# 320 series of products of zeros ahead of a hybrid decoder step: what distances of the operands modulo 512 bytes cost

## The chip, the cores and the metric

The kernel runs on one core of one Trainium2 chip. The metric is the device time of one execution in microseconds (us). A core has TensorE (PE; matmuls, with a weight load ahead of each), VectorE (DVE), ScalarE (ACT), GpSimd (POOL) and SyncE (SP, which issues most DMAs). Operands lie in SBUF, in 128 partitions; products go to PSUM.

## The reference

One inference step of a hybrid decoder trunk with one layer, for a prompt of 512 tokens and 8 samples of 8 tokens, 576 tokens in all with 1024 features:

```python
u = _rms(x) * g_pre_mix
proj = u @ w_in                                   # Mamba2-SSD heads and mLSTM heads, one projection
...
x = x + _rms(mix) * g_post_mix
u = _rms(x) * g_pre_x                             # cross attention to a memory of 256 rows
...
x = x + _rms(o) * g_post_x
u = _rms(x) * g_pre_ffn
f = (jax.nn.silu(u @ w_gate) * (u @ w_up)) @ w_down
x = x + _rms(f) * g_post_ffn
```

It returns the new x of both groups, the memory's keys and values, and the states of the scans. All of it is in float32.

## The kernel before

All activations are held with features on partitions and the 576 tokens along the free dimension, eight tiles of 128 features each. To keep float32 accuracy, both the activation and the weight of a large product are split into a rounded high part and a low part (type float32r), and a product is made of three matmuls: high weight by high activation, high weight by low activation, low weight by high activation. The 576 tokens are taken in two parts, either 256 and 320 or 288 and 288; the products of values per token are 512 wide, with the activation as the 128-column operand and the weight as the moving one.

`build` writes the layer down in order, and a scheduler settles the order of the instructions on each engine by its own simulation, within the constraints that the code gives (`issue_after`, `high_priority`, `manual_schedule`, which fixes the written order).

What stands around the change is the beginning. Line 300 clears a small tile `wz`; line 303 issues 21 products of it (`ps_warm`), which nobody reads; line 304 loads the parameters. Then the eight feature tiles of x are loaded, and ScalarE and VectorE make their high parts `uh` (L322) and low parts `ul` (L323) as they come, and `split` (L191, L192) does the same for the two first weight tiles, `whi` and `wlo`. The first stage, lines 339 to 341, multiplies them as they become ready: 8 feature tiles by 2 weight tiles by 2 parts of the tokens by 3 matmuls, 96 products:

```python
mm(ps, wh, ah, start=k == 0, stop=False)
mm(ps, wh, al, start=False, stop=False)
mm(ps, wl, ah, start=False, stop=k == KT - 1)
```

Behind it `gemm` (L202, L203, L205) does the same for the other tiles of the projection, and the later stages follow: values (L815), output projection (L202 to L205, `ps_o`), cross attention, and the feed-forward products (L1846 to L1848).

`SL(slot, ...)` takes one of the large slots of SBUF, 18,432 bytes in each partition; slot 1 is first used by `qk` (L470) in the kernel before. `MP` takes one of three rotating PSUM tiles, of one bank each.

Of the kernel before, what the change touches and what calls it, by code (L numbers as in the profile page):

```python
# [11 lines left out]
F32 = mybir.dt.float32  # L12
F32R = mybir.dt.float32r
# [6 lines left out]
P = 128  # L20
# [95 lines left out]
def build(nc, tc, ctx, I, O):  # L116
    V, A, G, S, TE = nc.vector, nc.scalar, nc.gpsimd, nc.sync, nc.tensor
    mm = TE.matmul
# [12 lines left out]
    def SL(slot, name, dt=F32, shape=(P, KT, T)):  # L131

        return big.tile(list(shape), dt, name=name, tag="s%d" % slot, bufs=1)
# [5 lines left out]
    def MP(name="m"):  # L139
        return pa.tile([P, 512], F32, name=name, tag="a")  # L140
# [54 lines left out]
    def gemm(ps, units, xh, xl, t0, n, k0=0, k1=None, order=None, late=0):  # L195


        tiles = [(hi[:, j * P:(j + 1) * P], lo[:, j * P:(j + 1) * P]) for hi, lo, nk in units for j in range(nk)]
        order = order or range(len(tiles))
        for i, k in list(enumerate(order))[k0:k1]:  # L200
            (wh, wl), ah, al = tiles[k], xh(k, t0, n), xl(k, t0, n)
            mm(ps, wh, ah, start=i == 0, stop=False)  # L202
            mm(ps, wh, al, start=False, stop=False)  # L203
            for c in range(late) if i == late - 1 else [i] if i >= late else ():
                m = mm(ps, tiles[order[c]][1], xh(order[c], t0, n), start=False, stop=c == len(tiles) - 1)  # L205
        return m
# [94 lines left out]
    psw = MP("ps_warm")  # L301
    for _ in range(NWARM):
        mm(psw[:, 0:256], wz[:, 0:128], wz, start=True, stop=True, skip_group_check=True)
    S.dma_start(par, I["par"])

    wi = [[wp.tile([P, 1024], F32R, name=k, tag=k, bufs=3) for k in ("whi", "wlo")] for _ in range(2)]
# [46 lines left out]
    stop = gemm(ps0[2][1], [(*w2, KT)], U, UL, 256, 320, 0, NSS)  # L353
# [12 lines left out]
    stop = gemm(ps0[3][0], [(*w3, KT)], U, UL, 0, 256)  # L366
# [343 lines left out]
    for g in range(2):  # L710
        psb = BP("ps_ls")
        pb3 = psb.rearrange("p (h t) -> p h t", h=8)
        for h in range(8):
            mm(psb[:, h * TS:(h + 1) * TS], sel[:80, 8 * g + h:8 * g + h + 1].to_broadcast([80, P]), cumst[:, TP:T],
               start=h == 0, stop=h == 7, skip_group_check=True)
# [8 lines left out]
        for h in range(8):  # L724
            k, j = h % 2, (8 * g + h) // 2
            mm(psi[64 * k:64 * k + 64, j * TS:(j + 1) * TS], xdts[:, 8 * g + h, :], lm[:, h, :], start=True, stop=True,
               skip_group_check=True)
# [12 lines left out]
    for b in range(4):  # L740
# [3 lines left out]
        for g in range(2):  # L744
            for hb in (1, 0):
# [3 lines left out]
                   start=b == 0, stop=b == 3, skip_group_check=True)  # L749
        for hb in range(2):  # L750
            bb, hn, (bst, xst) = 4 * hb + b, hns[hb], hbs[hb]
            bm = sd.tile([96, 256], F32R, name="bm", tag="bm", bufs=1)
# [136 lines left out]
    for h in range(4):  # L889
        q, k = qk[:, h, :], qk[:, 4 + h, :]  # L890
# [5 lines left out]
        dm = mp_.tile([P, 512], F32, name="dm", tag="dm", bufs=2)  # L896
# [5 lines left out]
        for c in range(4):  # L902
            mm(pss[:, c * P:(c + 1) * P], k[:, c * P:(c + 1) * P], q[:, c * P:(c + 1) * P], start=True, stop=True,
               skip_group_check=True)
# [39 lines left out]
    for h in range(4):  # L944
        mm(psb[:, h * TS:(h + 1) * TS], sel[:68, h:h + 1].to_broadcast([68, P]), sxst[:, TP:T], start=h == 0, stop=h == 3,
           skip_group_check=True)
# [22 lines left out]
    for hb in range(2):  # L969
# [6 lines left out]
        for b in range(4):  # L976
# [3 lines left out]
            for h in range(4):  # L980
                mm(psn[32 * h:32 * h + 32, 0:257], qpad[:, h, bb, :], c0[:, h, 0:257], start=False, stop=b == 3,
                   skip_group_check=True)
# [241 lines left out]
    x = SL(1, "x1")  # L1224
# [267 lines left out]
    def xo(j, i, pool=None):  # L1492

        t0, n = EHALVES[i]

        with tc.issue_after(evx[j - 3].ins if j > 2 else ovs[5].ins):
            ps, w = GP("ps_xo")[:, :n], weights(("xo", j), I["wxo"][j], pool=pool, cut=1024)

        def step(k0, k1):
            m = gemm(ps, [(*w, KT)], act(oh), act(ol), t0, n, k0, k1, [2, 3, 4, 5, 6, 7, 0, 1], 6 if j == 3 else 0)  # L1500
            if k1 < KT:
                return m
            add_sq(ph, ssq, ps, j if i == 0 else XO1.index(j), n, t0=t0)
            evx.append(A.activation(f[:, j, t0:t0 + n], ps, AF.Copy, scale=PAR("g_postx", j)))
            return m, evx[-1]
        return step
# [10 lines left out]
    for j in range(8):  # L1517
        step = xo(j, 0, wx if 3 < j < 7 else None)
# [662 lines left out]
    parts = [(c, d) for c in range(2) for d in range(2)]  # L2181
# [172 lines left out]
```

## Time and profile before

| | |
|---|---|
| median of 2 runs | 1088.56 us (1088.47 to 1088.65) |
| the profiled execution | 1087.01 us, of which the span from the first to the last instruction is 1085.2 us |
| mean granted TensorE clock | 0.998 |
| instructions on PE | 8124 matmuls, 8124 weight loads |
| moved from and to HBM | 160.28 MB read, 20.65 MB written |

The span is what the profile shows of one execution. In its rows, PE is a matmul, PEld a weight load; the two overlap, and matmuls overlap each other as well, so that a row's duration is longer than the distance to the next row. "L202" is line 202 of the kernel; "ps_in<-uh,whi" names what is written and read; "x24" is a count. In the rows of stretches, an engine's count takes in every instruction that lies in the stretch with any part of it.

### The profile page before, as it was taken

The page shows a single profiled execution, that of the slowest core. Times are in us where ns is not written, and L with a number is a line of the kernel's source. Part 1 is how long each engine was busy: PE and PEld are TensorE (multiplying, and loading weights), DVE is VectorE, ACT ScalarE, POOL GpSimd, SP SyncE. Part 2 cuts the span into 40 slices and gives each one's busy share as a digit, 9 for nine tenths or more (in the row PEclk, how much of TensorE's full clock was granted, in tenths as well). Part 3 has the DMA queues.
Part 4 walks back from the last instruction along what each step waited for, and adds up shares of the span by engine and source line. Part 5 has one row for each costly group of instructions (what it writes and reads, how often), then busy time and mean ns, then how long its engine had stood idle before and what let it go on. Part 6 is the DMA issues. An engine that isn't in the chain of part 4 may idle for free.

```text
span 1085.2 us, 20708 instructions
## 1 busy us (share of the span) xinstructions
PE 1075.0 (99%) x8124; PEld 1022.1 (94%) x8124; DVE 752.4 (69%) x1507; ACT 610.9 (56%) x1098; POOL 228.0 (21%) x305
## 2 busy tenths in 40 slices
PE   9999999999999999999999999999999999999997
PEld 9999887778999999999999989999999999999997
DVE  6896785658877775568755546766467887787556
ACT  7867632355654555656555545645566566656653
POOL 1332643313113111000154301100011111111000
PEclk9999999999999999999999999999999999999999
DMA  6775535435654449653458775643486697578532
GB/s 211 179 159 126 161 111 172 165 80 185 190 152 144 110 123 324 226 193 101 152 194 288 271 252 180 239 133 92 135 176 137 159 203 163 117 189 184 125 131 88
DMA packets 58966, 182.29 MB, mean 168 GB/s; under 512 B 6604, under 2 KB 11852, under 8 KB 58356
## 3 DMA queue, kind: packets, MB, share of 16 engines
q1 hardware_dynamic: 42740, 138.06, 38.6%
q0 software_dynamic: 15552, 41.95, 19.6%
q8 instruction: 64, 1.05, 0.4%
q10 hardware_dynamic: 576, 0.95, 0.3%
q14 instruction: 34, 0.28, 0.1%
HBM read 160.28 MB, written 20.65 MB: 167 GB/s over the span
## 4 chain that ended last, share of the span: by engine, by line
PE 86%; DVE 5%; ACT 4%; issue 2%; DMA 2%; POOL 0%; DVEq 0%; SPq 0%; ACTq 0%; POOLq 0%
PE ps_in L203 4%; PE ps_in L202 4%; PE ps_in L205 4%; PE ps_v L815 3%; PE ps_o L205 3%; PE ps_o L203 3%; PE ps_g L1846 3%; PE ps_g L1847 3%; PE ps_o L202 3%; PE ps_u L1847 3%; PE ps_u L1848 3%; PE ps_u L1846 3%; PE ps_g L1848 3%; PE ps_dn L1846 2%; PE ps_dn L1847 2%
## 5 line engine op out<-in xcount | busy, mean ns | idle before, releaser
L202 PE MATMUL ps_in<-uh,whi 128*128 128x320 f32 (+1 forms) x544 | 162.9, 300 | 0.5 <-DVE cb L451 0.5
L205 PE MATMUL ps_in<-uh,wlo 128*128 128x320 f32 (+1 forms) x544 | 162.3, 299 | 0.3 <-DMA wlo<-win 0.3
L203 PE MATMUL ps_in<-ul,whi 128*128 128x320 f32 (+1 forms) x544 | 161.8, 298 | 0.0
L180 ACT CAST whi<-raw 128x1024 fp32r<-128x1024 f32 (+1 forms) x104 | 105.2, 1013 | 100.0 <-PE ps_in L203 25.9
L187 DVE TENSOR_TENSOR wlo<-raw,whi 128x512 fp32r<-128x512 f32 (+1 forms) x96 | 93.7, 978 | 75.1 <-ACT whi L180 74.0
L202 PEld LDWEIGHTS ps_in<-uh,whi 128*128 128x128 f32 x544 | 102.8, 189 | 3.3 <-issue 1.7
L205 PEld LDWEIGHTS ps_in<-uh,wlo 128*128 128x128 f32 x544 | 102.3, 188 | 1.5 <-DMA wlo<-win 0.5
L203 PEld LDWEIGHTS ps_in<-ul,whi 128*128 128x128 f32 x544 | 102.4, 188 | 0.6
L185 POOL DMA_DIRECT2D wlo<-win x32 | 27.8, 869 | 80.7 <-ACT wlo L184 70.0
L1847 PE MATMUL ps_g<-b,whi 128*128 128x288 f32 x144 | 42.5, 295 | 0.0
L1846 PE MATMUL ps_g<-b,whi 128*128 128x288 f32 x144 | 42.4, 295 | 0.0
L1847 PE MATMUL ps_u<-b,whi 128*128 128x288 f32 x144 | 42.4, 295 | 0.0
L1846 PE MATMUL ps_u<-b,whi 128*128 128x288 f32 x144 | 42.2, 294 | 0.0
L1819 ACT CAST whi<-rawx 128x1024 fp32r<-128x1024 f32 (+1 forms) x26 | 25.6, 984 | 27.9 <-PE ps_dn L1847 13.8
L192 DVE TENSOR_TENSOR wlo<-sw,whi 128x1024 fp32r<-128x1024 f32 (+1 forms) x26 | 29.6, 1140 | 14.9 <-ACT whi L191 14.8
L202 PE MATMUL ps_xo<-qh,whi 128*128 128x288 f32 x128 | 38.5, 303 | 0.2 <-ACT whi L180 0.2
L205 PE MATMUL ps_o<-mixm_h,wlo 128*128 128x256 f32 (+1 forms) x128 | 37.9, 296 | 0.0
L1798 ACT CAST whi<-raw 128x1024 fp32r<-128x1024 f32 (+1 forms) x26 | 25.6, 983 | 21.8 <-PE ps_g L1847 9.7
L203 PE MATMUL ps_xo<-ql,whi 128*128 128x288 f32 x128 | 37.8, 296 | 0.0
L205 PE MATMUL ps_o<-mixs_h,wlo 128*128 128x320 f32 (+1 forms) x128 | 37.7, 295 | 0.0
L203 PE MATMUL ps_o<-mixs_l,whi 128*128 128x320 f32 (+1 forms) x128 | 37.7, 295 | 0.0
L203 PE MATMUL ps_o<-mixm_l,whi 128*128 128x256 f32 (+1 forms) x128 | 37.7, 295 | 0.0
(769 smaller groups left out, 3853.6 us busy)
## 6 DMA issues: line engine op xcount, KB each, us to landing
raw<-win SPq DMA_DIRECT2D x35, 512.0 KB, 4.0
raw<-wout SPq DMA_DIRECT2D x17, 512.0 KB, 3.7
raw<-wxq SPq DMA_DIRECT2D x13, 512.0 KB, 6.0
raw<-wgate SPq DMA_DIRECT2D x13, 512.0 KB, 3.6
raw<-wup SPq DMA_DIRECT2D x13, 512.0 KB, 5.1
wlo<-win POOLq DMA_DIRECT2D x24, 256.0 KB, 5.1
kva<-vc SPq DMA_DIRECT2D x11, 512.0 KB, 5.0
raw<-wv SPq DMA_DIRECT2D x10, 512.0 KB, 4.0
```

Source lines behind the costliest of these rows:

```text
L180: casts.append(A.copy(hi[:, :n], raw[:, :n]))
L185: G.dma_start(lo[:, a:b], src[:, a:b], accum_op=ALU.add)
L187: e.tensor_tensor(lo[:, a:b], raw[:, a:b], hi[:, a:b].bitcast(F32), op=ALU.subtract)
L192: (eng or V).tensor_tensor(lo, src, hi.bitcast(F32), op=ALU.subtract)
L202: mm(ps, wh, ah, start=i == 0, stop=False)
L203: mm(ps, wh, al, start=False, stop=False)
L205: m = mm(ps, tiles[order[c]][1], xh(order[c], t0, n), start=False, stop=c == len(tiles) - 1)
L815: mm(ps, a, b, skip_group_check=True, **kw)
L1798: s.c1 = A.copy(s.h1[:, s.all], s.r1[:, s.all])
L1846: mm(ps, wh, b[0][k], start=start and k == 0, stop=False, skip_group_check=True)
L1847: mm(ps, wh, b[1][k], start=False, stop=False, skip_group_check=True)
L1848: m = mm(ps, wl, b[0][k], start=False, stop=k == nk - 1, skip_group_check=True)
```

## The change

Ahead of the load of the parameters, VectorE clears a tile `bench` of 4608 float32 elements in each partition (slot 1), and PE is given 320 segments of products of it. All go to one PSUM tile, which nobody reads. Nothing is removed, and no other line is touched.

```diff
     for _ in range(NWARM):
         mm(psw[:, 0:256], wz[:, 0:128], wz, start=True, stop=True, skip_group_check=True)
+
+    bench = SL(1, "bench", F32R, (P, 4608))
+    V.memset(bench.bitcast(F32), 0.0)
+    SEG = []
+    for a in (0, 16, 32, 48):
+        for bm in range(8):
+            for dm in range(8):
+                if dm < 4 or not 0 <= a // 16 + (bm + 4) % 8 - 4 < 4:
+                    SEG.append((a, bm, dm, 576, ((320, 12), (256, 12), (320, 12), (256, 12), (288, 18), (512, 9))))
+    for a in (0, 16):
+        for bm in range(8):
+            for dm in range(8):
+                SEG.append((a, bm, dm, 288, ((288, 24),)))
+    pq = MP("ps_probe")
+    with tc.manual_schedule(engines={TE.engine}):
+        for a, bm, dm, step, parts in SEG:
+            for n, count in parts:
+                for i in range(count):
+                    k = i // 3 % (4 if step == 576 else 8)
+                    x = 64 + step * k + (a + 16) % 64 + (16 * bm + (1024 if step == 576 else 1152) if i % 3 == 1 else 0) + (256 if n == 320 else 0)
+                    w = 3600 + (16 * dm + 384 if i % 3 == 2 else 0)
+                    if n == 512:
+                        mm(pq[:, 0:n], bench[:, x:x + P], bench[:, w:w + n], start=i < 1, stop=True, skip_group_check=True)
+                    else:
+                        w += 128 * (k % 4)
+                        mm(pq[:, 0:n], bench[:, w:w + P], bench[:, x:x + n], start=i < 1, stop=True, skip_group_check=True)
     S.dma_start(par, I["par"])
```

Each segment copies the pattern of the kernel's own products, three at a time (i % 3): weights at w with the operand at x, the same weights with a second operand, other weights with the first operand. An element has 4 bytes, so 16 elements are 64 bytes and 128 are 512. Modulo 512 bytes, `a` sets the place of the first operand against the weights, `bm` that of the second operand against the first, `dm` that of the second weights against the first, each in steps of 64 bytes. The step of 576 or 288 elements from one threesome to the next moves the operand by 256 or 128 bytes modulo 512. At 512 columns the roles are exchanged: 128 columns at x are loaded as weights, and 512 from w are streamed.

The diff moves the later lines down by 26: L339 of before is L365 after.

## Prediction

> **What bounds the kernel now.** I read the page first: the span, the busy shares and the chain that ended last.
>
> ```profile
> span 1085.2 us, 20708 instructions
> ...
> PE 1075.0 (99%) x8124; PEld 1022.1 (94%) x8124; DVE 752.4 (69%) x1507; ACT 610.9 (56%) x1098; POOL 228.0 (21%) x305
> ```
> ```profile
> PE 86%; DVE 5%; ACT 4%; issue 2%; DMA 2%; POOL 0%; DVEq 0%; SPq 0%; ACTq 0%; POOLq 0%
> ```
>
> TensorE (PE) is occupied 1075.0 of 1085.2 us and holds 86% of the chain, so the first question is whether it has gaps in which further products could run. The view of waits, restricted to PE, answers it; these are its three longest.
>
> ```profile
> PE ps_warm L303 <- DVE wz L300: 1.1, 1, 1.1
> PE ps_in L202 <- DVE cb L451: 0.5, 1, 0.5
> PE ps_in L205 <- DMA wlo<-win: 0.3, 1, 0.3
> ```
>
> Behind the start, no wait is longer than 0.5 us. There is no gap to hide anything in: whatever is put into PE's queue ahead of the first stage moves all that follows by its own length. So the prediction is a count of products times the pace at which PE takes them.
>
> The pace has to be read with care. Busy time divided by the count would be wrong, since matmuls overlap: a row of the timeline shows how long one product was under way, but the next starts well before that has passed. The pace is the distance from start to start. Here are pairs of rows of PE's timeline, the first row of a series of equal products and the row that follows its last.
>
> ```profile
> 461.93 0.28 PE L202 MATMUL ps_o<-mixm_h,whi 128*128 128x256 f32 x1
> ...
> 464.75 0.31 PE L202 MATMUL ps_o<-mixm_h,whi 128*128 128x320 f32 x1
> ...
> 468.27 0.31 PE L202 MATMUL ps_o<-mixm_h,whi 128*128 128x320 f32 x1
> ...
> 471.50 0.28 PE L228 MATMUL ps_ss<-c,ssqm 128*128 128x1 f32 x2
> ...
> 841.23 0.29 PE L1846 MATMUL ps_g<-b,whi 128*128 128x288 f32 x1
> ...
> 842.82 0.29 PE L1848 MATMUL ps_dn<-hh,wlo 128*128 128x288 f32 x1
> ...
> 236.16 0.39 PE L815 MATMUL ps_v<-whi,uh 128*128 128x512 f32 x1
> ...
> 237.08 0.39 PE L633 MATMUL ps_l<-cumst,c 80*128 80x512 bf16 x1
> ```
>
> From 461.93 to 464.75 lie 24 products of 256 columns: 2.82 us / 24 = 117.5 ns each, although one is under way for 280 ns. From 468.27 to 471.50 lie 22 of 320 columns: 146.8 ns. From 841.23 to 842.82 lie 12 of 288: 132.5 ns. From 236.16 to 237.08 lie 4 of 512: 230 ns. Each such product has its own weight load of 128 columns (the page counts 8124 of both), and the added ones are of the same kind: same type, 128 rows, weights loaded anew for each. I chose series in the middle of what the trace shows. For the ends I took the slowest and the fastest clean series (without a pause) of each size, and two long stretches.
>
> ```profile
> 485.79:488.51 2.72, 2.72 (x26) 1.00 0.53 188
> 1062.86:1065.00 2.14, 2.14 (x20) 1.00 0.14 50
> 398.24:401.71 3.47, 3.47 (x27) 1.00 0.40 120
> 1046.54:1049.22 2.68, 2.68 (x21) 1.00 0.21 89
> 865.40:866.57 1.17, 1.17 (x11) 1.00 0.83 305
> 962.19:963.40 1.21, 1.21 (x11) 1.00 0.17 29
> 235.25:236.16 0.91, 0.91 (x5) 1.00 0.11 36
> 198.64:200.04 1.40, 1.40 (x8) 1.00 0.45 181
> 743.90:850.00 106.10, 106.10 (x805) 1.00 0.59 137
> 401.00:441.00 40.00, 40.00 (x306) 1.00 0.90 306
> 5.37:18.59 13.22, 13.22 (x98) 1.00 0.95 335
> ```
>
> The columns are the stretch, its length, PE's busy time and count, the granted clock, the DMA share and GB/s. The count takes in the one to three products that were still under way at the first edge; those that start in the eight short stretches are 24, 18, 24, 18, 9, 9, 4 and 6. So 256 columns went at 113.3 to 118.9 ns, 320 at 144.6 to 148.9, 288 at 130.0 to 134.4, 512 at 227.5 to 233.3. The clock stood at 1.00 in all of them.
>
> **The change part by part.** *The products.* The list has 192 segments with a step of 576 (for a distance dm below 4 all 4 x 8 x 4 = 128; for dm of 4 and more the condition keeps 4 of 8 values of bm, 4 x 4 x 4 = 64) and 2 x 8 x 8 = 128 with a step of 288. A segment of the first kind issues 24 products of 320 columns, 24 of 256, 18 of 288 and 9 of 512; one of the second kind issues 24 of 288. That makes 4608 of 320, 4608 of 256, 3456 + 3072 = 6528 of 288, and 1728 of 512: 17,472 products with 5,419,008 columns, twice what the whole kernel had. At the middle paces: 4608 x 117.5 = 541.4 us, 4608 x 146.8 = 676.5, 6528 x 132.5 = 865.0, 1728 x 230 = 397.4, in all 2480.3 us. With every size at its fastest row: 522.1 + 666.3 + 848.6 + 393.1 = 2430.1. With every size at its slowest: 547.9 + 686.1 + 877.4 + 403.1 = 2514.5. Nothing lies beside them that counts: they are on the path with their full length. I take the middle, because the long stretch from 743.90 to 850.00, whose products are of 288 columns but for one in four of 256 or 320, gives 106.10 us / 803 = 132.1 ns, in the middle too.
>
> *The memset of bench and the first stage.* VectorE fills 4608 elements in each partition ahead of its first real work, and the products of zeros wait for it. No memset of that size is in the trace. The nearest row of VectorE is
>
> ```profile
> L1730 DVE TENSOR_TENSOR f_xo<-f_xo 128x1152 f32<-128x1152 f32 x4 | 5.4, 1358 | 0.1
> ```
>
> that is four times 1152 elements in 5.4 us, so at most about 5.4 us from the end of the small memset, which the timeline of the start puts at 1.06; if it goes faster, it is over before PE has done its warm-up.
>
> ```profile
> 1.06 4.66 PE L303 MATMUL ps_warm<-wz 128*128 128x256 bf16 x21 [1.06 <-DVE wz L300]
> 5.37 0.56 PE L339 MATMUL ps_in<-uh,whi 128*128 128x256 f32 x1
> 5.74 0.42 PE L340 MATMUL ps_in<-ul,whi 128*128 128x256 f32 x1
> 5.95 0.67 PE L339 MATMUL ps_in<-uh,whi 128*128 128x320 f32 x2
> 6.43 0.31 PE L340 MATMUL ps_in<-ul,whi 128*128 128x256 f32 x1
> 6.58 0.31 PE L339 MATMUL ps_in<-uh,whi 128*128 128x320 f32 x1
> ```
>
> In the changed program's order PE's queue holds the warm-up, three real products of L339 (which need only ScalarE's rounded parts), then all products of zeros, then the other 93 products of the first stage. So the zeros start between 5.95 and 6.5. What is queued behind PE's wait for the memset is the whole rest of its work, but it is late by at most 0.5 us. In return, 93 products find all operands ready: at the middle paces they take 93 x 132.2 = 12.3 us, where the 96 of before needed 13.22 us from 5.37 to 18.59 (last row of the windows). The first stage then ends at about 6.5 + 2480.3 + 12.3 = 2499.1 instead of 18.59: 2480.5 later; with a quick memset 0.5 less. The order of the other engines differs in a handful of steps near the start, and of the main products only within the first stage; the loads, splits and squares of that stage do not need PE and are done beside the zeros. Behind them PE finds its next weights ready, which can save the short waits named above, 0.8 us. I set all of that at nothing beyond the 0.2 us.
>
> *The sum.* Profiled execution: 1085.2 + 2480.5 = 3565.7 us of span. The execution itself took 1087.01, 1.8 us more than its span, and the median of before is 1088.56, another 1.55. So 3565.7 + 1.8 + 1.55 = 3569 us.
>
> **Rivals.** *A: distances that the trace doesn't have are dear.* The change varies the places of the operands modulo 512 bytes through all multiples of 64, and the tuned kernel has only some of them. Rows of one shape differ: 113.3 and 118.9 for 256 columns. If every untried distance were as far above the slowest row as that is above the fastest, the paces would be 124.5, 153.2, 138.8 and 239.1 ns, the added time 573.7 + 705.9 + 906.1 + 413.2 = 2598.9, the total 3687 us. Against it: the stretch of 803 products from 743.90 runs over several weight and operand tiles at different places and still comes out at 132.1 ns. The Trainium skill (TensorE: Matmul & The Clock Gate, Part 2, Step-by-step: what each phase is for) says that weights and moving operand come through two read ports of their own, so that loading doesn't slow the running product; by that, no distance would matter. The spread from 113.3 to 118.9 ns does not refute it, nor does it bear it out. I give A 7%, for a time above 3604.
>
> *B: only the columns cost.* The products of zeros run beside idle engines and nearly idle DMA. If the surplus over the bare columns came from their traffic, it would go. The least price of a column that rows give is (227.5 - 118.9) / 256 = 0.424 ns, which makes 2299 us for 5,419,008 columns and a total of 3388 us. Against it: the stretch from 401.00 to 441.00 has the highest DMA share but the first stage, 0.90, and its products, half of 256 and half of 320 columns, take 40 us / 304 = 131.6 ns, no more than elsewhere; the slowest rows of 256 and 320 stand at DMA shares of 0.14 and 0.21. The Trainium skill (same page, Back-to-back issue gap) gives N / 2.4 + 2.5 ns from start to start for N columns once the clock is up: an estimate of 109 ns for 256 and 2302 us for all, a total of 3390 us. The trace disagrees, 117.5 ns. 4%.
>
> *C: zeros don't keep the clock.* The 21 warm-up products of zeros took 4.66 us, some 212 ns for 256 columns, before PE reached its pace. If the zeros ran on like that, 5,419,008 x 212 / 256 = 4488 us come on top: 5576 us. Against it: the sixth real product already starts 0.15 us behind the fifth (6.43 to 6.58), so the clock came up on a history that was nearly all zeros. 2%.
>
> *D, not slower: the products never run.* Nobody reads what they write, and something between program and chip might drop them. Then only the memset is left, at most 5.4 us ahead of VectorE's first step: 1089 to 1094 us. It decides if the count of products in the trace stays at 8124. Against it: nobody reads the warm-up either, and it stands in the row above with all its 21. 1%.
>
> **How the numbers follow.** The forecast has 86%: 3569 us, from 1088.56 + 2430.1 - 1.8 = 3517 (all paces at their fastest, and the short waits gone) to 1088.56 + 2514.5 + 1 = 3604. That already holds more than 8 in 10, so the range is 3517 to 3604 and reaches into no rival. What a measurement of this kernel can tell from no change is about 2%. Only D lies within it: 1%; none is faster; forecast, A, B and C make 99% slower.
>
> **What the profile after would show.** The span about 3566 us with 25,596 products and as many weight loads; PE busy 99% or more; the added lines in groups of 15,744 and 1,728 products, whose mean duration again says nothing of their pace; DMA near 0 GB/s, VectorE, ScalarE and GpSimd idle from about the first to the twenty-eighth of 40 slices, with one wait on PE of some 2.4 ms for each. The start of the first 320-column series to that of the next segment should be 10.8 us (24 x 264.3 ns + 18 x 132.5 + 9 x 230), for every segment of the first kind; A is right if some segments take 11.3 us or more, B if all take about 10. Behind the zeros the stages should be as long as before, from the end of the first stage 1085.2 - 18.6 = 1066.6 us to the end. I am wrong if the pace differs by more than 2% for most distances, if the granted clock leaves 1.00, or if PE pauses among the zeros to fetch instructions; in the stretch from 743.90, 803 products ran without a pause that shows.

## The result, and the profile after

The changed kernel takes 3569.16 us (median of 2 runs, 3568.42 to 3569.91), 3.279 times the time before (95% interval 3.274 to 3.285). The forecast was 3569.

The profiled execution took 3569.91 us, 3568.1 of it span. Its page, to be set beside the one of before:

```profile
span 3568.1 us, 55657 instructions
...
PE 3557.6 (100%) x25596; PEld 3429.1 (96%) x25596; DVE 756.0 (21%) x1508; ACT 611.0 (17%) x1098; POOL 227.0 (6%) x305
...
DVE  2000000000000000000000000000767767565875
ACT  1000000000000000000000000000735555455665
POOL 0000000000000000000000000000342211311110
PEclk9999999999999999999999999999999999999999
...
GB/s 63 1 1 1 1 1 1 1 1 1 1 1 1 1 1 1 1 1 1 1 1 1 1 1 1 1 1 1 136 148 142 160 207 149 270 183 138 163 168 118
```

PE has 17,472 matmuls more than before (25,596 against 8124) and is hardly ever idle; the other engines stand still for 27 of the 40 slices, and DMA moves 1 GB/s. Their busy times in us are those of before, within 4. The view of waits says the same from the other side: each engine has one wait of the length of the zeros.

```profile
DVE wlo L187 <- ACT whi L180: 2553.8, 50, 2478.0
POOL rx_y L239 <- DVE rx_v L238: 2484.1, 1, 2484.1
ACT xs L388 <- PE ps_in L367: 2477.6, 1, 2477.6
```

The start of PE's timeline shows where the zeros begin, and the stretches show how long each part is (length, then busy time and count of PE, PEld, DVE, ACT and POOL, then clock, DMA share and GB/s).

```profile
5.62 1.06 PE L365 MATMUL ps_in<-uh,whi 128*128 128x256 f32 x3
6.48 0.72 PE L329 MATMUL ps_probe<-bench 128*128 128x320 f32 x3
```
```profile
6.48:2489.32 2482.84, 2482.84 (x17473) 2407.29 (x17473) 14.84 (x26) 12.46 (x22) 1.72 (x12) 1.00 0.01 3
2489.32:2501.53 12.21, 12.21 (x96) 12.21 (x94) 0.00 (x0) 1.02 (x2) 0.00 (x0) 1.00 0.00 0
2501.53:3568.10 1066.57, 1057.10 (x8009) 1005.75 (x8007) 736.40 (x1478) 593.75 (x1068) 224.30 (x283) 1.00 0.59 166
```

The zeros run from 6.48 to 2489.32: 2482.84 us for 17,472 products. The rest of the first stage takes 12.21 us. From there to the end are 1066.57 us; in the kernel before, the same stretch has

```profile
18.59:1085.20 1066.61, 1057.45 (x8009) 1005.88 (x8007) 740.19 (x1484) 597.20 (x1073) 226.06 (x292) 1.00 0.59 166
```

1066.61 us, with the same 8009 products. All that was added lies ahead of 2501.53, and nothing behind it moved but as a whole.

Worked out from the starts of all products, by size: 256 columns 543.0 us (117.8 ns each), 320 columns 675.3 (146.6), 288 columns 864.2 (132.4), 512 columns 400.3 (231.6). The segments with a step of 576 take 10.65 to 10.95 us (forecast 10.8). These are the cheapest and the dearest of them, each 75 products (the row counts one still under way at the edge):

```profile
1433.43:1444.38 10.95, 10.95 (x76) 1.00 0.01 1
1887.99:1898.64 10.65, 10.65 (x76) 1.00 0.01 2
```

The first is a=32, bm=5, dm=4, with 256 columns at 119.8 to 121.2 ns; the second a=48, bm=4, dm=2, with 113.3 ns. So the distances do matter, by up to 7% at 256 columns, but the mean over them hardly differs from the middle of the rows of before. One more thing stands in these numbers: segments that differ only by 4 in bm or dm, that is by 256 bytes, mostly have the same time: 119 of 128 such pairs agree within 0.01 us. The pattern repeats every 256 bytes, not every 512.

### The profile page after: what moved, and what is told of

Read it like the earlier page. It is cut to its first block, busy times and chain, and to the rows that moved or that the text cites. A ratio compares the mean times of both kernels' runs of the same rounds, so it can differ in the third digit from the quotient of the medians.

```text
span 3568.1 us, 55657 instructions
## 1 busy us (share of the span) xinstructions
PE 3557.6 (100%) x25596; PEld 3429.1 (96%) x25596; DVE 756.0 (21%) x1508; ACT 611.0 (17%) x1098; POOL 227.0 (6%) x305
## 4 chain that ended last, share of the span: by engine, by line
PE 95%; DVE 1%; ACT 1%; DMA 1%; issue 1%; POOL 0%; DVEq 0%; ACTq 0%; POOLq 0%
PE ps_probe L329 58%; PE ps_probe L326 11%; PE ps_in L203 1%; PE ps_in L202 1%; PE ps_in L205 1%; PE ps_v L841 1%; PE ps_o L205 1%; PE ps_o L203 1%; PE ps_g L1872 1%; PE ps_g L1873 1%; PE ps_o L202 1%; PE ps_g L1874 1%; PE ps_u L1874 1%; PE ps_u L1873 1%; PE ps_u L1872 1%
## 5 line engine op out<-in xcount | busy, mean ns | idle before, releaser
L329 PEld LDWEIGHTS ps_probe<-bench 128*128 128x128 f32 x15744 | 2104.2, 188 | 16.8
L329 PE MATMUL ps_probe<-bench 128*128 128x288 f32 (+2 forms) x15744 | 2114.0, 295 | 0.0
L326 PE MATMUL ps_probe<-bench 128*128 128x512 f32 x1728 | 431.4, 394 | 0.0
L326 PEld LDWEIGHTS ps_probe<-bench 128*128 128x128 f32 x1728 | 313.9, 188 | 58.8
L180 ACT CAST whi<-raw 128x1024 fp32r<-128x1024 f32 (+1 forms) x104 | 105.4, 1013 | 104.1 <-PE ps_in L203 32.5
```

The source lines that it names most:

```text
L180: casts.append(A.copy(hi[:, :n], raw[:, :n]))
L326: mm(pq[:, 0:n], bench[:, x:x + P], bench[:, w:w + n], start=i < 1, stop=True, skip_group_check=True)
L329: mm(pq[:, 0:n], bench[:, w:w + P], bench[:, x:x + n], start=i < 1, stop=True, skip_group_check=True)
```

## The experiments

Theory T, behind the prediction: a product costs a pace that its size and the distances of its operands set, whatever lies in the operands and whatever other engines do; the paces add up with full length on the path. Each version but the last was run once, beside runs of the kernel before (medians of 1088.1 to 1088.6 us).

**One cheap place, one dear place.** If distances set the pace, a segment taken alone must keep its time when all others are like it.

```diff
+    SEG = [(48, 4, 2, s, p) if s == 576 else (0, 3, 5, s, p) for _, _, _, s, p in SEG]
     pq = MP("ps_probe")
```

> All 320 segments at one place each: the 192 of step 576 at a=48, bm=4, dm=2, whose segment took 10.653 us in the changed kernel (256 columns at 113.3 ns), the 128 of step 288 at a=0, bm=3, dm=5 (131.2 ns). Theory T (a product's pace is set by its size and by the distances, and comes out the same each time): 192 x 10.653 + 128 x 24 x 131.2 ns = 2448 us of zeros instead of 2482.8, 3535 us in all. Rival H (the differences between segments come from what ran before them, not from the distances): about the mean, 2483 us of zeros, 3569 us.

```diff
+    SEG = [(32, 5, 4, s, p) if s == 576 else (16, 7, 2, s, p) for _, _, _, s, p in SEG]
     pq = MP("ps_probe")
```

> The same with the dearest places: a=32, bm=5, dm=4 (10.954 us a segment, 256 columns at 119.8 to 121.2 ns) and a=16, bm=7, dm=2 (133.6 ns). Theory T: 192 x 10.954 + 128 x 24 x 133.6 ns = 2514 us of zeros, 3600 us in all. Rival H: 2483 and 3569 us.

Measured: 3536.16 and 3602.97 us. The stretches of the zeros, first of the cheap place, then of the dear one:

```profile
7.01:2455.23 2448.22, 2448.22 (x17473) 1.00 0.01 2
```
```profile
6.06:2522.10 2516.04, 2516.04 (x17474) 1.00 0.01 3
```

2448.22 against 2448 by T, and 2516.04 against 2514; H wanted 2483 for both. The 192 cheap segments took 10.653 us each, to 0.001 but for the first, which took 10.670. The dear ones took 10.967, not 10.954: they settle only in the second segment, so what ran just before has a small say.

**Reverse order.** How large that say is, the same segments in the other order tell.

```diff
+    SEG = SEG[::-1]
     pq = MP("ps_probe")
```

> The same 320 segments in reverse order. Theory T: 2483 us of zeros, and every segment of a place has its time of before within some 0.02 us. Rival H: also about 2483 us, but the segments of a place take other times, with a scatter like that between places (0.05 us).

Measured: 3571.12 us, with the zeros, the dearest and the cheapest place at

```profile
6.63:2489.23 2482.60, 2482.60 (x17473) 1.00 0.01 3
```
```profile
1051.19:1062.14 10.95, 10.95 (x77) 1.00 0.00 0
596.85:607.50 10.65, 10.65 (x76) 1.00 0.01 2
```

The two places keep their times to 0.01 us. Over the 192 segments with a step of 576 the difference to the changed kernel has a scatter of 0.024 us, and the times correlate at 0.87. So T holds for the sum, while up to a quarter of the variance between places (0.024 squared over 0.049 squared) goes with the order. The profiled execution took 1.2 us more than that of the changed kernel, and this lies behind the zeros.

**One segment.**

```diff
+    SEG = SEG[:1]
     pq = MP("ps_probe")
```

> The first segment alone, and the memset whole. Theory T (all the time is products, the memset of 3.9 us and the changed start cost nothing): one segment of 10.9 us on top of 1088.6, with the zeros starting at 6.5 us and 93 products behind them at 132 ns: 1099 to 1100 us. A rival that puts a part of the time into the memset and the start: some 4 us more, 1104 us.

Measured: 1097.62 us, 9.5 more than the kernel before, run beside it (1088.11), and 1.4 less than T's range. The stretches of the segment and of the 93 products behind it are

```profile
6.33:17.15 10.82, 10.82 (x78) 1.00 0.93 292
17.15:29.46 12.31, 12.31 (x95) 1.00 0.20 74
```

The first stage ends at 29.46 instead of 18.59: 10.87 later. The span is 1095.8 us, 10.6 more than in the profile of before, so the segment is on the path with its length. T's range was reckoned from 1088.6 us, while the profiled execution of before took 1087.01; runs of the kernel before differ by that much (1087.58 to 1089.37 in 15 of them). The memset and the changed start cost nothing that can be seen.

**Values instead of zeros.**

```diff
-    V.memset(bench.bitcast(F32), 0.0)
+    S.dma_start(xraw, I["xT"])
+    A.copy(bench, xraw.rearrange("p k t -> p (k t)"))
```

> bench is filled with the input x (one load and one copy by ScalarE) instead of zeros; the products are the same in number, size and place. Theory T: the same paces, 2483 us of products, and a start some 10 to 20 us later, since x must be loaded first: 3580 to 3590 us. Rival Z (zeros are cheap, values cost clock): granted clock below 0.99 and over 2530 us of products.

Measured: 3579.39 us. The products took

```profile
13.54:2498.95 2485.41, 2485.41 (x17472) 1.00 0.01 3
```

2485.41 us with the granted clock at 1.00 over the whole stretch, and by size the same means as zeros for 288 and 512 columns to 0.01 ns. Nearly all of the 2.6 us more lies at the very front, in PE's timeline:

```profile
13.54 4.85 PE L330 MATMUL ps_probe<-bench 128*128 128x320 f32 x18 [7.83 <-ACT bench L307]
```

PE had waited 7.83 us for the data. Of its next 24 products, the 320-column ones started 267 ns apart (the first took 431) and the 256-column ones 213 ns, half the pace; then it was back. The stretches give the clock, the first for these 4.85 us, the second for the products behind:

```profile
13.54:18.39 4.85, 4.84 (x19) 0.50 0.91 267
20.20:2498.95 2478.75, 2478.75 (x17444) 1.00 0.01 2
```

So the granted clock was 0.50 there: this is rival C's price, paid for 24 products behind a pause and not for what the operands hold. Rival Z is out: behind that start, values cost no more than zeros.

**Traffic beside the zeros.**

```diff
+    busy = sp.tile([P, 1152], F32, name="busy")
+    fill = [sp.tile([P, 1024], F32, name="fill%d" % j) for j in range(2)]
+    V.memset(busy, 0.0)
     pq = MP("ps_probe")
-    with tc.manual_schedule(engines={TE.engine}):
+    with tc.manual_schedule(engines={TE.engine, V.engine, S.engine}):
         for a, bm, dm, step, parts in SEG:
+            if step == 576:
+                for j in range(6):
+                    V.tensor_tensor(busy, busy, busy, op=ALU.add)
+                for j in range(2):
+                    S.dma_start(fill[j], I["win"][j])
```

> Beside the zeros VectorE adds a tile of 1152 columns to itself 1152 times, and SyncE loads 384 weight tiles of 512 KB into a tile that nobody reads. Theory T: the products take 2483 us as before. Rival B, turned round (the traffic of other engines sets the surplus over the columns): the products beside the traffic are slower by 1% or more, 2508 us or more in all.

Measured: 3569.67 us. Here are 493 us of the zeros, first with traffic, then the same products in the changed kernel without it:

```profile
7.00:500.00 493.00, 493.00 (x3428) 475.23 (x3427) 480.31 (x373) 15.14 (x27) 4.04 (x11) 1.00 0.79 241
```
```profile
7.62:500.62 493.00, 493.00 (x3428) 475.23 (x3427) 13.70 (x22) 11.73 (x21) 1.72 (x12) 1.00 0.02 8
```

VectorE is busy 480 us instead of 14, DMA moves 241 GB/s instead of 8, and PE takes the same 3428 products in the same time. The loads lasted until 871 us and the additions until 1627; over all, the zeros took 2482.83 us against 2482.84. The traffic of others is not where the surplus over the columns comes from.

**Half the weight columns.** Then perhaps the loads of the weights, which run beside the product ahead.

```diff
-                        mm(pq[:, 0:n], bench[:, w:w + P], bench[:, x:x + n], start=i < 1, stop=True, skip_group_check=True)
+                        mm(pq[0:64, 0:n], bench[:, w:w + 64], bench[:, x:x + n], start=i < 1, stop=True, skip_group_check=True)
```

(and likewise at 512 columns).

> Every added product loads 64 weight columns instead of 128, and writes 64 partitions; the streamed columns stay. If the surplus over the bare columns and the differences between distances come from the weight load that reads beside the running product (theory W): 256 columns fall from 117.8 to 113 ns or less, the scatter between places goes down, the sum falls to 2350 to 2430 us, in all about 3480. If they are a fixed price of a product (rival F): 2483 us of products, 3569 us.

Measured: 3552.36 us, and for the products

```profile
6.51:2469.40 2462.89, 2462.89 (x17475) 1.00 0.01 3
```

20 us or 0.8% less: 256 columns went from 117.8 to 116.7 ns, not to 113, although a weight load now takes 134 ns and not 188:

```profile
L329 PEld LDWEIGHTS ps_probe<-bench 128*64 128x64 f32 x15744 | 2014.2, 134 | 88.6
```

As the main cause of the surplus, theory W falls; F is nearer, though not exact. For the differences between places it is otherwise: the scatter of the 192 segments went from 0.049 to 0.039 us, and their times correlate with those of the changed kernel at only 0.31, where the reverse order had 0.87. The cheapest place stayed the cheapest (10.62 us), but the dearest fell to 10.74, and a=32, bm=3, dm=3 is now the dearest with 10.81. Which place is dear thus hangs in part on the width of the weights, in the load or in what is written.

**Two bytes instead of four.** What was left was the type of the operands.

```diff
-    bench = SL(1, "bench", F32R, (P, 4608))
-    V.memset(bench.bitcast(F32), 0.0)
+    bench = SL(1, "bench", BF16, (P, 4608))
+    V.memset(bench, 0.0)
```

> bench holds bfloat16 instead of float32r: the same numbers of products and columns, half the bytes, and all distances halved with them. What is left open is the surplus over the columns, which half the weight columns did not take away. Theory R (the surplus and the differences between distances are a matter of reading 4-byte elements): the products go at nearly one price per column, 0.42 ns by the row-derived least price of the prediction, 109 to 112 ns for 256 columns, 2290 to 2350 us in all the products, 3380 to 3440 us. Rival F (a fixed price of any product): 2483 us, 3569 us.

Measured: 3389.61 us. The stretch of the products, and the groups of the weight loads (of the changed kernel, then of this one):

```profile
6.50:2308.11 2301.61, 2291.56 (x17283) 1709.37 (x17473) 14.36 (x24) 12.78 (x22) 1.73 (x12) 1.00 0.01 3
```

```profile
L329 PEld LDWEIGHTS ps_probe<-bench 128*128 128x128 f32 x15744 | 2104.2, 188 | 16.8
```
```profile
L329 PEld LDWEIGHTS <-bench 128*128 128x128 bf16 x15744 | 1540.4, 98 | 424.1
```

The products took 2301.6 us, 7.3% less. From start to start 256 columns now take 109.2 ns, 288 take 122.5, 320 take 135.8 and 512 take 215.9, and 9 in 10 starts lie within 1 ns of that: the differences between distances are gone with the surplus (the changed bytes halve all distances, but there are still many of them). A weight load takes 98 ns instead of 188. The numbers are those of theory R: the surplus goes with float32r, and bfloat16 doesn't have it. That it lies in the reading of the operands, and not elsewhere in such a product, is not shown by this run. (The trace lacks 192 records of 512-column products, one in each segment; the stretch is timed by its ends.) This is also the one price of rival B, 3388 us, reached by another cause than B gave.

**The table used on the kernel itself.** The kernel before has most of its products of 256 and 320 columns at a=48, bm=0, dm=0. The cheapest place differs from it by 128 bytes of the low weights. This version leaves out the zeros and moves the low weight tiles by 128 bytes modulo 256, with small tiles of the Newton steps in between, so that of the large tiles only the raw weights move with them, which PE doesn't read.

```diff
     nv = ctx.enter_context(tc.tile_pool(name="newton", bufs=1))
+    wl = ctx.enter_context(tc.tile_pool(name="lows", bufs=1))
+    na = ctx.enter_context(tc.tile_pool(name="newton_a", bufs=1))
+    wq = {"whi": wp, "wlo": wl}
...
-        hi, lo = [(pool or wp).tile([P, 1024], F32R, name=k, tag=k, bufs=NWX if pool else 3) for k in ("whi", "wlo")]
+        hi, lo = [(pool or wq[k]).tile([P, 1024], F32R, name=k, tag=k, bufs=NWX if pool else 3) for k in ("whi", "wlo")]
...
-        a = nv.tile(shape, F32, name=name + "_a", tag="nt_a", bufs=2)
+        a = na.tile(shape, F32, name=name + "_a", tag="nt_a", bufs=2)
...
```

> The kernel before, without any zeros; the low weight tiles lie 128 bytes further from the high ones modulo 256 (other small tiles take the place between). By the zeros' own table (theory T carried over) 397 threesomes of 256 columns go from 114.8 to 113.3 ns a product, 348 of 320 from 146.4 to 145.6, 116 of 288 from 133.0 to 131.3: 3 to 5 us less, 1084 to 1085.5 us. If the zeros' table doesn't carry over to the kernel's own products: 1088.6 us, within 1.

Measured, in 11 runs: 1086.29 us against 1088.24 of the kernel before, ratio 0.9983 (0.9974 to 0.9992). That is 0.9 to 2.8 us less, 1.95 by the medians and not the 3 to 5 expected: the table carries over, with about half the gain. Two series of its timeline, the same stage as in the prediction's rows:

```profile
456.11 0.28 PE L205 MATMUL ps_o<-mixm_h,whi 128*128 128x256 f32 x1
...
458.83 0.30 PE L205 MATMUL ps_o<-mixm_h,whi 128*128 128x320 f32 x1
...
462.32 0.28 PE L205 MATMUL ps_o<-mixm_h,whi 128*128 128x256 f32 x1
```

24 products of 256 columns in 2.72 us, 113.3 ns instead of 117.5; 24 of 320 in 3.49 us, 145.4 instead of 146.8. Over the kernel, the threesomes at that place went from 115.8 to 114.4 ns (256 columns), 146.8 to 145.6 (320) and 132.6 to 132.1 (288). But 102 threesomes of 320 columns at another place lost, from 144.9 to 146.3 ns, 0.4 us in all, and PE waits longer for others: the waits behind the start add up to 2.8 us instead of 1.8.

```profile
PE ps_in L205 <- DVE cb L454: 0.8, 1, 0.8
PE ps_h L619 <- POOL xe L617: 0.5, 1, 0.5
PE ps_in L205 <- DVE cb L456: 0.4, 1, 0.4
```

## Why the prediction was right

**The bound.** PE had no gap, and the zeros cost their full length: 2482.84 us of zeros against 2480.6 us of difference between the medians.

**The terms.** Forecast and measured, in us: 256 columns 541.4 and 543.0; 320 columns 676.5 and 675.3; 288 columns 865.0 and 864.2; 512 columns 397.4 and 400.3; sum 2480.3 and 2482.8. Each is within 0.8%, and part of that cancels. That the total came out within 0.2 us is luck: the span was 2.4 us longer than forecast (3568.1 against 3565.7), while the profiled execution lay 0.75 us above the median and not 1.55 below it as before. The sum was good because the pace was read from start to start. Read from the mean durations of the rows (280, 309, 295 and 394 ns in the profile after, by size) it would have come to 5.3 ms. The 512 columns were the weakest term: 230 ns came from four products, two of them with 64 weight columns. (The added columns are 2.4 times those of the kernel before, 2,274,544 by its trace, and not twice; no term rests on that.)

**The start.** The zeros were expected between 5.95 and 6.5 and started at 6.48. The memset took 3.9 us where the row of VectorE's additions had bounded it by 5.4:

```profile
1.91 3.90 DVE L306 MEMSET bench<- 128x4608 f32 x1 [0.91 <-issue]
```

It did not bind: the three real products ahead started late, at 5.62, because ScalarE's parts came late (the first piece of `whi` at 5.57, against 5.29 before). The 93 products took 12.21 us (forecast 12.3), and the way to the end 1066.57 us (forecast 1066.6). Net, the start was worth 0.2 us in the forecast and about nothing in the runs.

**Rival A** (untried distances dear) had its mechanism half right: distances matter, by a fixed amount for each place that the runs of the cheap and of the dear place repeated to about 0.1%. Its size was wrong. The dearest place costs 1.3% more than the mean, not 5%, and the places of the kernel before had already shown nearly both ends, 113.3 and 118.9 ns at 256 columns. So its time could at most be that of the dear place, 3603 us, and the mean over places lay at the middle.

The rule named there, that the weight load reads through a port of its own (the Trainium skill, TensorE: Matmul & The Clock Gate, Part 2), is not borne out for float32r: only the places of the weights and operands differ between segments, and 256 columns go from 113.3 to 121.2 ns; and with 64 weight columns instead of 128 other places became the dear ones. With bfloat16 no distance was seen to matter, as the rule has it.

**Rival B** (only the columns cost) failed on its cause: the run with traffic and the stretch without it agree to 0.01 us in 2482.8. The rule beside it (the Trainium skill, same page, Back-to-back issue gap: N / 2.4 + 2.5 ns, given there for an isolated product, without a budget for weight loads) is right to 0.2 ns for bfloat16, 109.2 ns at 256 columns and 215.9 at 512, and 9 to 16 ns too low for float32r, 117.8 and 231.6.

**Rival C** (zeros at half clock) failed: the granted clock was 1.00, and only the first product of zeros still had the pace of the warm-up, 266 ns to the next start. Half the clock showed only in the run with values, behind a wait of 7.83 us. **Rival D** (the products never run) failed: the trace counts all 17,472, though nobody reads their result.

## What to carry to other kernels

When PE is the bound and never waits, an addition costs count times pace, and the pace is the distance from one start to the next in a clean series of the same size and type; the duration in the row is 1.7 to 2.4 times too long here. Take the pace from the rows of the kernel itself and not from a rule for another type: by float32r's pace the same products in bfloat16 would have been forecast 8% too long, and the other way round 7% too short. Where float32r products are the bound, the places of weights and operands modulo 256 bytes were worth up to 7% of the time of a product of 256 columns and 2.8% of a whole segment; here the better place of one family of tiles was worth 1.95 us of 1088.

## What the runs showed that was not expected

- The surplus over bfloat16's pace goes with float32r. At 256, 288, 320 and 512 columns float32r took 117.8, 132.4, 146.6 and 231.6 ns, bfloat16 109.2, 122.5, 135.8 and 215.9. The differences (8.7, 9.9, 10.7 and 15.7 ns before rounding) grow with the columns, 7 to 8% at each size, so that most of the surplus is no fixed price of a product as rival F had it. Halving the weight columns took away 1.2 ns of the 8.7 at 256 columns, the traffic of other engines nothing. What in float32r costs it stays open: no run took the operand's and the weights' types apart, nor the reading of them from the multiplying.
- The places act mostly with a period of 256 bytes. The first weights lay at the same place modulo 512 bytes in all segments, so the runs do not tell an operand's distance from them from its own place. The same place gives the same time to a thousandth of a microsecond in the run with one cheap place (10.653 us for 191 of 192 segments). A place may take two times, depending on what ran before: the dear one 10.954 or 10.967 us.
- After a pause of 7.8 us ahead of the products, the granted clock was 0.50 and the next 24 went at half the pace (267 ns at 320 columns, 213 at 256).
